# The low-rank gate of GLA moves to the start of the kernel and into four column groups; RWKV matmuls alternate between row groups

## The chip, the cores and the metric

The kernel runs on one core of one Trainium2 chip. The metric is the device time of one execution in microseconds (us). Names of engines in the traces: PE is TensorE (PEld its weight loads), DVE is VectorE, ACT is ScalarE, POOL is GpSimd, SP is the queue that issues the loads and stores.

## The reference

One layer of a hybrid decoder with 1024 tokens and model width 1024, all in fp32. One normalised input is projected once and its columns go to three token mixers, whose outputs (256 + 512 + 256 columns) go into one output projection; a SwiGLU feed-forward part and a last norm follow.

```python
hn = rms_norm(x, norm1_g[l])
p_rw, p_lru, p_gla = _split(hn @ w_in[l], (RW_PROJ, LRU_PROJ, GLA_PROJ))
y_rw = rwkv7_mixer(p_rw, ...)
y_lru = rglru_mixer(p_lru, ...)
y_gla = gla_mixer(p_gla, ...)
x = x + jnp.concatenate([y_rw, y_lru, y_gla], axis=-1) @ w_out[l]
hn = rms_norm(x, norm2_g[l])
x = x + (jax.nn.silu(hn @ ffn_w_gate[l]) * (hn @ ffn_w_up[l])) @ ffn_w_down[l]
```

Two places of the mixers matter here. RWKV takes decay and rate from two low-rank inputs of 64 columns each:

```python
w_raw = w0 + jnp.tanh(w_lo) @ w_up
decay = jnp.exp(-RW_DECAY_SCALE * jax.nn.sigmoid(w_raw.astype(f32)))
a = jax.nn.sigmoid(a0 + a_lo @ a_up)
```

GLA takes its gate from a low-rank input of 16 columns, `gk_lo`, which is one of the slices of the common projection:

```python
q, k, v, gk_lo, g = _split(p, GLA_SIZES)
log_a = jax.nn.log_sigmoid((gk_lo @ gk_up + gk_b).astype(f32)) / GLA_GATE_NORM
```

## The kernel before

Channels lie on the 128 partitions and tokens along the rows. The sequence is taken in two halves of 512 tokens (h = 0, 1). A half is loaded as eight tiles of 128 channels (`ys[h]`), each is multiplied by the norm's weights g1 and split into a high and a low part (xh, xl, in the type fp32r) by `split_x`; 1/rms of each token (`rstd`) is multiplied in only when a result is copied out of PSUM. Weights are split in the same way (wh, wl). A projection of 128 columns is 24 matmuls of 128x512: wh with xh, wh with xl and wl with xh, for eight tiles of channels (`mm3`, line L133). These are most of the kernel's matmuls, and fill TensorE between the mixers' own.

The mixers are functions that issue their instructions step by step in the order of the list `ORDER`. A step is a letter and a number: R is the projection of RWKV, H its output gate's, l and L projection and mixer of the LRU, P and G projection and mixer of GLA, and for the four groups of RWKV (256 tokens each) a is `rw_prep`, b `rw_inner`, c `rw_chain`, p `rw_post`. S splits the second half, O and F are the output projection of half 0 and the LRU's last norm. `AHEAD` gives steps a priority. A scheduler then puts each engine's instructions in a fixed order from dependences, priorities and its own estimate of durations, so that the order of a step's matmuls in the code is not the order in which they stand on TensorE.

What the change touches: `gla_proj` computes the 16 gate columns with 16 matmuls of 128x32 in fp32r (L504 with xh, L505 with xl; the 32 columns hold the high and the low part of the weights, `wgh`), copies them into the first 32 rows of the tile `sc`, and `gla_mix` multiplies by `gku`, which holds gk_up twice (L518). `rw_prep` computes decay from rows 0 to 63 of `ups` and `pw` (L301, two matmuls of 256 columns) and rate from rows 64 to 127 (L309). `rw_inner` computes scores (L368) and transposes B and K by eight matmuls for each half of the rows (L378). Each of these writes into a bank of PSUM named pi, of which there are two; projections mostly use two banks named mm.

Near the mixers' end there are three chains. The LRU's last norm takes a statistic (L174) for each tile and a division and gelu with table loads on ScalarE (L661, L663), then VectorE (L666) and a cast (L104). RWKV's last group ends with the output gate's matmul (L488), VectorE's product (L489), a cast and a subtraction (L104, L105). Then the output projection of half 1 adds x (reloaded from `x1d` at L826), and a statistic (L813) starts the norm ahead of the feed-forward part (first matmul L861).

## Time and profile before

| | |
|---|---|
| median of 3 runs | 1205.6 us (1205.58 to 1206.74) |
| profiled execution, whole time | 1207.51 us |
| its span | 1205.7 us |
| TensorE clock granted, mean | 0.992 |
| TensorE busy | 1159.4 us, 96% |
| weight loads busy | 906.5 us, 75% |
| VectorE busy | 820.5 us, 68% |
| ScalarE busy | 557.5 us, 46% |
| GpSimd busy | 182.6 us, 15% |

The table is of one execution, whose whole time is 1.8 us more than its span. Startup takes the first 42 us or so, the mixers with their projections go on to 486 us, the output projection of half 1 to 534.5 us, and the feed-forward part starts at 538.83 us. In a timeline a matmul's busy time overlaps the next one's, so the distance from start to start is its price. Brackets behind a row tell how long the engine stood idle before it and which instruction ended the wait.

### The profile page before, as it was taken

The page shows a single profiled execution, that of the slowest core. Times are in us where ns is not written, and L with a number is a line of the kernel's source. Part 1 is how long each engine was busy: PE and PEld are TensorE (multiplying, and loading weights), DVE is VectorE, ACT ScalarE, POOL GpSimd, SP SyncE. Part 2 cuts the span into 40 slices and gives each one's busy share as a digit, 9 for nine tenths or more (in the row PEclk, how much of TensorE's full clock was granted, in tenths as well). Part 3 has the DMA queues.
Part 4 walks back from the last instruction along what each step waited for, and adds up shares of the span by engine and source line. Part 5 has one row for each costly group of instructions (what it writes and reads, how often), then busy time and mean ns, then how long its engine had stood idle before and what let it go on. Part 6 is the DMA issues. An engine that isn't in the chain of part 4 may idle for free.

```text
span 1205.7 us, 18433 instructions
## 1 busy us (share of the span) xinstructions
PE 1159.4 (96%) x6550; PEld 906.5 (75%) x6550; DVE 820.5 (68%) x1513; ACT 557.5 (46%) x972; POOL 182.6 (15%) x141
## 2 busy tenths in 40 slices
PE   8899999999999999988899899999999999999996
PEld 4676667677776677766788778888888878888886
DVE  6878797887759676378978664356655475555775
ACT  7445734864541457365433234333333344444542
POOL 0000000000000000000036455454555400000000
PEclk9999999999999999999999999999999999999998
DMA  9865444343333268873699853245454798665422
GB/s 312 291 231 194 141 147 133 90 157 108 130 123 96 87 219 290 273 258 114 190 324 341 283 194 99 96 131 186 146 176 152 268 357 296 196 194 171 128 88 70
DMA packets 125213, 225.52 MB, mean 187 GB/s; under 512 B 13985, under 2 KB 17345, under 8 KB 125121
## 3 DMA queue, kind: packets, MB, share of 16 engines
q1 hardware_dynamic: 124432, 223.78, 55.1%
q8 instruction: 51, 0.84, 0.3%
q10 hardware_dynamic: 688, 0.57, 0.1%
q14 instruction: 42, 0.34, 0.1%
HBM read 149.84 MB, written 74.45 MB: 186 GB/s over the span
## 4 chain that ended last, share of the span: by engine, by line
PE 62%; DVE 15%; ACT 10%; DMA 9%; issue 3%; SPq 1%; POOL 0%; DVEq 0%; ACTq 0%; POOLq 0%
PE mm L861 24%; PE mm L1124 17%; PE mm L133 12%; DVE x L854 2%; DMA x<-w_dn_dram 2%; DMA wd<-x 1%; PE pi L368 1%; DMA wr<-w_in_dram 1%; DMA wr<-w_gu_dram 1%; ACT L663 1%; DVE wl L105 1%; PE pi L408 1%; DVE x L822 1%; DMA parts<-wl 1%; DVE u L651 1%
## 5 line engine op out<-in xcount | busy, mean ns | idle before, releaser
L133 PE MATMUL mm<-xl,wh 128*128 128x512 f32 x420 | 169.6, 404 | 0.0
L133 PE MATMUL mm<-xh,wh 128*128 128x512 f32 x400 | 162.8, 407 | 3.8 <-ACT wh L104 2.9
L133 PE MATMUL mm<-xh,wl 128*128 128x512 f32 x400 | 163.0, 408 | 0.3 <-DVE wl L105 0.3
L104 ACT CAST wh<-wr 128x512 fp32r<-128x512 f32 x133 | 82.0, 619 | 126.5 <-PE mm L861 37.7
L104 ACT CAST vh<-wr 128x512 fp32r<-128x512 f32 x81 | 50.2, 622 | 103.7 <-PE mm L1124 39.1
L133 PEld LDWEIGHTS mm<-xh,wh 128*128 128x128 f32 x400 | 75.4, 188 | 27.1 <-issue 6.1
L133 PEld LDWEIGHTS mm<-xl,wh 128*128 128x128 f32 x420 | 79.0, 188 | 21.9 <-issue 6.4
L105 POOL TENSOR_TENSOR wl<-wr,wh 128x512 fp32r<-128x512 f32 x36 | 53.0, 1472 | 279.9 <-ACT wh L104 265.2
L133 PEld LDWEIGHTS mm<-xh,wl 128*128 128x128 f32 x400 | 75.3, 188 | 22.6 <-issue 5.8
L1124 PE MATMUL mm<-ft,wh 128*128 128x512 f32 x264 | 81.5, 389 | 0.0
L1124 PE MATMUL mm<-ft,vh 128*128 128x512 f32 x264 | 81.3, 389 | 0.0
L854 DVE TENSOR_TENSOR x<-x 128x512 f32<-128x512 f32 x71 | 57.8, 824 | 29.2 <-DMA x<-hd 15.8
L105 DVE TENSOR_TENSOR wl<-wr,wh 128x512 fp32r<-128x512 f32 x97 | 66.3, 685 | 14.2 <-ACT wh L104 13.7
L417 POOL MEMSET ri<- 128x256 f32 x8 | 2.5, 312 | 391.3 <-DVE ri L402 389.3
L1124 PEld LDWEIGHTS mm<-ft,wh 128*128 128x128 f32 x264 | 49.6, 188 | 10.3
L1124 PEld LDWEIGHTS mm<-ft,vh 128*128 128x128 f32 x264 | 49.5, 188 | 10.2
L105 POOL TENSOR_TENSOR vl<-wr,vh 128x512 fp32r<-128x512 f32 x36 | 50.6, 1406 | 37.6 <-ACT vh L104 36.1
L1124 PE MATMUL mm<-ft,wl 128*128 128x512 f32 x132 | 51.3, 389 | 0.0
L1124 PE MATMUL mm<-ft,vl 128*128 128x512 f32 x132 | 51.3, 389 | 0.0
L104 ACT CAST wh<-ws 128x512 fp32r<-128x512 f32 x33 | 20.4, 622 | 50.9 <-PE mm L861 41.0
L105 POOL TENSOR_TENSOR wl<-ws,wh 128x512 fp32r<-128x512 f32 x27 | 38.4, 1424 | 34.6 <-ACT wh L104 26.9
L105 POOL TENSOR_TENSOR vl<-ws,vh 128x512 fp32r<-128x512 f32 x27 | 37.2, 1376 | 35.7 <-ACT vh L104 35.7
(498 smaller groups left out, 2901.0 us busy)
## 6 DMA issues: line engine op xcount, KB each, us to landing
wr<-w_gu_dram SPq DMA_DIRECT2D x108, 256.0 KB, 3.1
parts<-wh SPq DMA_DIRECT2D x60, 256.0 KB, 3.1
parts<-wl SPq DMA_DIRECT2D x60, 256.0 KB, 3.1
wh<-parts SPq DMA_DIRECT2D x57, 256.0 KB, 2.7
wl<-parts SPq DMA_DIRECT2D x57, 256.0 KB, 2.9
wr<-w_in_dram SPq DMA_DIRECT2D x44, 256.0 KB, 3.9
x<-w_dn_dram SPq DMA_DIRECT2D x44, 256.0 KB, 4.5
wd<-x SPq DMA_DIRECT2D x44, 256.0 KB, 3.9
```

The costliest lines, as they stand in the source:

```text
L104: S.copy(out=hi, in_=src)
L105: lo_eng.tensor_tensor(out=lo, in0=src, in1=hi.bitcast(F32), op=ALU.subtract)
L133: PE.matmul(out=ps, lhsT=ww[:, kk], rhs=xx(k), start=first, stop=last)
L368: PE.matmul(out=pgs[hh][:, n * P : n * P + P], lhsT=BKn[hs(hh), nn, 64 * hh : 64 * hh + 128], rhs=ARn[hs(hh), nn], start=True, stop=True)
L408: PE.matmul(out=ps[hs(hh), n * w : n * w + w], lhsT=lhs(hh, n), rhs=rhs(hh, n), start=True, stop=True)
L417: G.memset(hi(Zt), 0.0)
L651: V.tensor_tensor_scan(out=tt[j], data0=out(i), data1=ig[j], initial=lstate[:, i : i + 1], op0=ALU.mult, op1=ALU.add)
L663: S.activation(out=gate, in_=gate, func=AF.Exp, scale=-0.5)
L822: V.scalar_tensor_tensor(out=xk, in0=xk, scalar=vc("g2", k), in1=rs, op0=ALU.mult, op1=ALU.mult)
L854: eng.tensor_tensor(out=out, in0=a, in1=b, op=op)
L861: PE.matmul(out=ps, lhsT=ww[:, kk], rhs=xx, start=first and kk + i == 0, stop=kk == len(xc) - 1 and i == 2, skip_group_check=True)
L1124: PE.matmul(out=out(m), lhsT=ww[:, m], rhs=xx, start=first and open_(m) and k + i == 0, stop=k == KF - 1 and i == 2, skip_group_check=True)
```

## The change

The gate's projection becomes a function of its own, `gk_proj`, with a step "g": g0 stands first in `ORDER`, g1 right behind R1. It takes x itself in fp32, not its split parts, with weights that are multiplied by g1 once (L190). The eight tiles of channels go into four column groups of 32 columns, so two matmuls add up in each group, and the sum over the four groups is left to `gku`, which now holds gk_up four times in 128 rows. `sc` is used in all its rows, so the zeros that it needs in one corner are written after each use, in `gla_mix`. Loads grow from 64 to 128 KB (w_gk) and from 16 to 64 KB (gku). In `rw_prep` and `rw_inner` both banks are taken at once and the matmuls are issued in turn from the two halves of the rows.

```diff
 ORDER = (
-    "R0 H0 a0 l00 b0 k0 l01 a1 L00 c0 l02 X1 P0 b1 p0 "
-    "G0 l03 S1 L01 R1 a2 F0 c1 b2 p1 l10 H1 a3 l11 "
+    "g0 R0 H0 a0 l00 b0 k0 l01 a1 L00 c0 l02 X1 P0 b1 p0 "
+    "G0 l03 S1 L01 R1 g1 a2 F0 c1 b2 p1 l10 H1 a3 l11 "
     "l13 P1 c2 b3 p2 L10 c3 l12 O0 p3 G1 L11 F1"
...
         ups = cp.tile([P, 512], F32, name="ups")
-        gku = cp.tile([32, P], F32, name="gku")
-        wgh = cp.tile([P, 8, 32], F32R, name="wgh")
+        gku = cp.tile([P, P], F32, name="gku")
+        wgk = cp.tile([P, NK, 32], F32, name="wgk")
         cdec = cp.tile([P, 4], F32, name="cdec")
...
             V.tensor_scalar(out=lgh, in0=vt[:, VEC["lg"] : VEC["lg"] + 4], scalar1=0.5, scalar2=None, op0=ALU.mult)
-            gr = rtt((8, 16))
-            nc.sync.dma_start(out=gr, in_=w_gk)
-            split(wgh[:, :, 0:16], wgh[:, :, 16:32], gr, V)
+            nc.sync.dma_start(out=wgk, in_=w_gk)
+            g1 = vt[:, VEC["g1"] : VEC["g1"] + NK].unsqueeze(2)
+            V.tensor_tensor(out=wgk, in0=wgk, in1=g1.to_broadcast([P, NK, 32]), op=ALU.mult)
 
...
             bonus = y[:, 0:2, 3 + o : 259 + o]
-            psw = prep_ps()
+            psw, psa = prep_ps(), prep_ps()
             for hp in range(2):
-                PE.matmul(out=psw[:, hp * 256 : hp * 256 + 256], lhsT=ups[0:64, hp * P : hp * P + P], rhs=pw[0:64, sl], start=True, stop=True)
+                for ps, r in ((psw, slice(0, 64)), (psa, slice(64, P))):
+                    PE.matmul(out=ps[:, hp * 256 : hp * 256 + 256], lhsT=ups[r, hp * P : hp * P + P], rhs=pw[r, sl], start=True, stop=True)
             sig, cs, av = rtt(), rtt(), rtt()
...
                 V.tensor_tensor_scan(out=cs[:, hp], data0=cc("rs64"), data1=sig[:, hp], initial=0.0, op0=ALU.mult, op1=ALU.add)
-            psa = prep_ps()
-            for hp in range(2):
-                PE.matmul(out=psa[:, hp * 256 : hp * 256 + 256], lhsT=ups[64:128, hp * P : hp * P + P], rhs=pw[64:128, sl], start=True, stop=True)
             for hp in range(2):
...
             BKt = rw.tile([P, 2, 8, 64], F32, name="BKt", bufs=2)
+            pbs = [prep_ps(), prep_ps()]
+            for n in range(8):
+                for hh in range(2):
+                    PE.transpose(out=pbs[hh][:, n * 64 : n * 64 + 64], in_=BKn[hs(hh), n, 64 * hh : 64 * hh + 128], identity=ident[hs(hh), hs(hh)])
             for hh in range(2):
-                pb = prep_ps()
-                for n in range(8):
-                    PE.transpose(out=pb[:, n * 64 : n * 64 + 64], in_=BKn[hs(hh), n, 64 * hh : 64 * hh + 128], identity=ident[hs(hh), hs(hh)])
-                S.copy(out=BKt[:, hh], in_=pb.rearrange("p (n i) -> p n i", i=64))
+                S.copy(out=BKt[:, hh], in_=pbs[hh].rearrange("p (n i) -> p n i", i=64))
 
...
 
+        def gk_proj(h, xs):
+
+            ps = pm.tile([P, HT], F32, name="mm")
+            for i in range(2):
+                for j in range(4):
+                    kk = 4 * i + j
+                    PE.matmul(out=ps[32 * j : 32 * j + 32], lhsT=wgk[:, kk], rhs=ys[h][:, kk, 3:], start=i == 0, stop=i == 1, tile_position=(0, 32 * j), skip_group_check=True)
+            V.tensor_tensor(out=sc.rearrange("p a b -> p (a b)"), in0=ps, in1=xs[2], op=ALU.mult)
+
         def gla_proj(xs, y):
...
             qk = unit("qk", (2, HT))
-            q, k, v, g, gk = qk[:, 0], qk[:, 1], [unit("v0"), unit("v1")], [y[:, 6, 3:], y[:, 7, 3:]], sc[0:32].rearrange("p a b -> p (a b)")
-            ps = pm.tile([P, HT], F32, name="mm")
-            for kk in range(NK):
-                PE.matmul(out=ps[0:32], lhsT=wgh[:, kk], rhs=xh[kk], start=kk == 0, stop=False)
-                PE.matmul(out=ps[0:32], lhsT=wgh[:, kk], rhs=xl[kk], start=False, stop=kk == NK - 1)
-            V.tensor_tensor(out=gk, in0=ps[0:32], in1=rstd[0:32], op=ALU.mult)
+            q, k, v, g, gk = qk[:, 0], qk[:, 1], [unit("v0"), unit("v1")], [y[:, 6, 3:], y[:, 7, 3:]], sc.rearrange("p a b -> p (a b)")
             proj(xs, 16, q)
...
             PE.matmul(out=ps, lhsT=gku, rhs=gk, start=True, stop=True)
+            G.memset(sc[64:128, :, 0:64], 0.0)
             z, e = unit(0), unit(1)
...
         sc = gl.tile([P, 4, P], F32, name="sc")
-        G.memset(sc[64:128, :, 0:64], 0.0)
         state = {"rw": rwS, "gl": glS}
...
                 E[f"xs{h}"] = split_x(h)
+            elif k == "g":
+                gk_proj(h, xs)
             elif k == "R":
...
         tiled(cols),
-        np.ascontiguousarray(w_in[:, 2560:2576].reshape(8, P, 16).transpose(1, 0, 2)),
+        np.concatenate([w_in[:, 2560:2576].reshape(8, P, 16).transpose(1, 0, 2), np.zeros((P, 8, 16), np.float32)], 2),
         np.concatenate([np.concatenate([f("rw_w_up"), f("rw_a_up")], 0), f("rw_g_up")], 1),
         lw,
-        np.concatenate([f("gla_gk_up")] * 2, 0),
+        np.concatenate([f("gla_gk_up"), np.zeros((16, P), np.float32)] * 4, 0),
         tiled(np.concatenate([f("w_out")[:768], swap(f("w_out")[768:], 0)], 0))[:, :, KO],
```

How the scheduler's order moves is seen at three places. The first is the start. VectorE takes the first results of RWKV's projection (pw for decay and rate, pk for keys) out of PSUM, mixes each with its shifted copy (rd), and subtracts low parts of weights (wl); before, from the first result on:

```order
L252 TENSOR_TENSOR pw<-pi,rstd 128x512
L275 TENSOR_TENSOR rd<-pw 128x512
L277 SCALAR_TENSOR_TENSOR pw<-rd,vt,pw 128x512
L252 TENSOR_TENSOR pk<-pi,rstd 128x512
L105 TENSOR_TENSOR wl<-wr,wh 128x512
L275 TENSOR_TENSOR rd<-pk 128x512
L105 TENSOR_TENSOR wgh<-rt,wgh 128x8x16
```

VectorE at the same place now:

```order
L252 TENSOR_TENSOR pw<-pi,rstd 128x512
L275 TENSOR_TENSOR rd<-pw 128x512
L252 TENSOR_TENSOR pk<-pi,rstd 128x512
L277 SCALAR_TENSOR_TENSOR pw<-rd,vt,pw 128x512
L190 TENSOR_TENSOR wgk<-wgk,vt 128x256
L105 TENSOR_TENSOR wl<-wr,wh 128x512
L275 TENSOR_TENSOR rd<-pk 128x512
L277 SCALAR_TENSOR_TENSOR pk<-rd,vt,pk 128x512
L504 TENSOR_TENSOR sc<-mm,rstd 128x512
```

The split of the gate's weights (wgh) is gone. Their product with g1 stands behind both first results and the mixing of pw, and the gate's result (sc) is copied out before the decay goes on. TensorE there now, from the last two of the 48 projections that need no gate (pi) on:

```order
L133 MATMUL pi<-xl_172,wh 128x512
L133 MATMUL pi<-xh_171,wl 128x512
L503 MATMUL mm<-y_100,wgk 32x512 x8
L133 MATMUL mm<-xh_143,wh 128x512
...
L133 MATMUL mm<-xh_151,wl 128x512
L302 MATMUL pi<-pw,ups 128x256 x4
L133 MATMUL mm<-xh_155,wh 128x512
```

Before, 12 projections stood between that last pi and L301. Now L503 comes first, nine projections are between it and decay and rate, and fifteen of the same 24 come behind.

The second place is the last pair of LRU tiles, on TensorE. L174 with a tile u is the statistic, `xl_5014` (before) and `xl_4997` (of the change) are low parts of its second tile's result, xh those of the input projections, L450 and L449 are RWKV's last chain. Before:

```order
L133 MATMUL mm<-xh_4282,wh 128x512
L174 MATMUL px<-u_4937,ct 128x512
L133 MATMUL mm<-xl_4283,wh 128x512
...
L133 MATMUL mm<-xh_4258,wh 128x512
L450 MATMUL pc<-R_4151,Tt 64x64 x4
L133 MATMUL mm<-xl_4259,wh 128x512
...
L133 MATMUL mm<-y_5004,wh 128x512
L465 MATMUL pp<-XR_3762,UV_3202 64x64
...
L133 MATMUL mm<-y_5004,wh 128x512
L133 MATMUL mm<-xl_5014,wh 128x512
```

Now:

```order
L133 MATMUL mm<-xl_4988,wh 128x512
L174 MATMUL px<-u_4910,ct 128x512
...
L133 MATMUL mm<-xl_4991,wh 128x512
L174 MATMUL px<-u_4920,ct 128x512
L133 MATMUL mm<-y_4987,wl 128x512
...
L133 MATMUL mm<-y_4987,wh 128x512 x2
...
L133 MATMUL pi<-y_4987,wl 128x512
L449 MATMUL pc<-R_4133,Tt 64x64 x4
L133 MATMUL mm<-y_4987,wh 128x512 x2
...
L133 MATMUL mm<-xl_4997,wh 128x512
```

Before, input projections (xh) stood behind both statistics, and 35 projections lay between the second one and the first instruction that needs its tile (the one ahead of `xl_5014`). Now the input projections are over ahead of the first statistic, and 22 projections, all of the output projection, stand between the second one and the first that needs its tile (the pair behind L449).

The third place is the output gate of RWKV's last group, on TensorE. `xl_5017` (before) and `xl_5000` (of the change) are the first tile that needs its result. Before:

```order
L133 MATMUL px<-y_5004,wh 128x512
L488 MATMUL pp<-pgl,ups 128x256 x2
L133 MATMUL px<-xl_5005,wh 128x512
L133 MATMUL px<-y_5004,wl 128x512
...
L133 MATMUL px<-y_5004,wl 128x512
L133 MATMUL mm<-y_5004,wh 128x512
L133 MATMUL mm<-xl_5017,wh 128x512
```

Now:

```order
L133 MATMUL px<-xl_4997,wh 128x512
L487 MATMUL pp<-pgl,ups 128x256 x2
L133 MATMUL px<-y_4987,wl 128x512
L133 MATMUL mm<-y_4987,wh 128x512 x2
L133 MATMUL pi<-y_4987,wh 128x512
L133 MATMUL mm<-xl_5000,wh 128x512
```

Before, 23 projections (px) stood between the gate and the first use of its result, now one. Behind it, the statistic ahead of the feed-forward part has 58 projections to cover its chain, where it had 60. The order of the feed-forward part is the same but for single rows.

## Rows read from the trace of the kernel before

**Rows 1.** Windows: length, busy (count) of PE, PEld, DVE, ACT, POOL, clock, DMA, GB/s.

```profile
42.00:486.00 444.00, 437.36 (x3320) 319.16 (x3320) 347.37 (x801) 233.07 (x391) 2.50 (x8) 1.00 0.48 159
486.00:540.00 54.00, 47.40 (x191) 35.53 (x192) 28.06 (x47) 24.45 (x39) 0.00 (x0) 0.98 0.79 280
...
32.80:36.00 3.20, 3.18 (x5) 1.68 (x6) 1.68 (x4) 0.90 (x2) 0.00 (x0) 0.50 1.05 392
```

**Rows 2.** Timeline of TensorE, first instruction of the feed-forward part.

```profile
538.83 0.76 PE L861 MATMUL mm<-q_b21h,vh 128*128 128x512 f32 x1 [4.18 <-ACT ft L803]
```

**Rows 3.** Timeline of TensorE near the start.

```profile
22.23 0.39 PE L133 MATMUL pi<-xh,wl 128*128 128x512 f32 x1
...
32.82 0.80 PE L133 MATMUL mm<-xh,wh 128*128 128x512 f32 x1 [2.74 <-ACT wh L104]
...
42.24 0.50 PE L133 MATMUL mm<-xh,wl 128*128 128x512 f32 x1 [0.35 <-DVE wl L105]
```

**Rows 4.** L504's weight loads (its line's view); two dense starts (timeline).

```profile
L504 PEld LDWEIGHTS mm<-xh,wgh x16: 107/108/112, 108.0 to 329.5; 128*32 128x32 f32 x16
...
112.67 0.39 PE L504 MATMUL mm<-xh,wgh 128*32 128x512 f32 x1
112.90 0.40 PE L505 MATMUL mm<-xl,wgh 128*32 128x512 f32 x1
```

**Rows 5.** Timeline of TensorE, decay and rate of group 0.

```profile
26.43 0.48 PE L301 MATMUL pi<-pw,ups 64*128 64x256 f32 x1 [0.77 <-ACT pw L279]
26.44 0.48 PE L309 MATMUL pi<-pw,ups 64*128 64x256 f32 x1
...
27.50 0.50 PE L133 MATMUL mm<-xh,wl 128*128 128x512 f32 x1
```

**Rows 6.** Timeline of TensorE, column groups (L578) and their follower.

```profile
167.40 0.32 PE L578 MATMUL px<-u 128*32 128x64 f32 x8
167.65 0.50 PE L133 MATMUL mm<-xh,wh 128*128 128x512 f32 x1
```

**Rows 7.** Timeline of VectorE, behind the four of pw and pk.

```profile
26.23 0.68 DVE L105 TENSOR_TENSOR wl<-wr,wh 128x512 fp32r<-128x512 f32 x1
```

**Rows 8.** Timeline of TensorE, decay and rate of group 1.

```profile
131.21 1.13 PE L301 MATMUL pi<-pw,ups 64*128 64x256 f32 x4 [1.10 <-DVE Tt L426]
132.27 0.50 PE L133 MATMUL mm<-xh,wl 128*128 128x512 f32 x1
...
133.86 0.70 PE L309 MATMUL pi<-pw,ups 64*128 64x256 f32 x2
...
134.87 0.70 PE L309 MATMUL pi<-pw,ups 64*128 64x256 f32 x2
```

**Rows 9.** Timeline of ScalarE, the copy that frees the second bank.

```profile
132.33 0.57 ACT L428 COPY MV<-pi 128x512 f32<-128x512 f32 x1
```

**Rows 10.** Timeline of TensorE, scores (L368) and transposes (L378).

```profile
72.61 1.71 PE L368 MATMUL pi<-AR,BK 64*128 64x128 f32 x16
...
174.88 0.71 PE L378 MATMUL pi<-ct,BK 64*128 64x64 f32 x8
...
377.29 1.02 PE L378 MATMUL pi<-ct,BK 64*128 64x64 f32 x16
```

**Rows 11.** Timelines of TensorE and ScalarE, the last LRU pair.

```profile
470.49 1.12 PE L174 MATMUL px<-u,ct 128*128 128x512 f32 x2
...
477.26 1.28 ACT L661 ACT_TABLE_LOAD   x1
...
481.95 0.62 ACT L104 CAST y<-y 128x512 fp32r<-128x512 f32 x1 [0.82 <-DVE y L666]
```

**Rows 12.** Timelines of TensorE, VectorE and ScalarE, the last gate.

```profile
495.93 1.03 PE L488 MATMUL pp<-pgl,ups 128*128 128x256 f32 x4
...
497.00 0.69 DVE L489 TENSOR_TENSOR y<-pp,ro 128x512 f32<-128x512 f32 x1 [1.26 <-PE pp L488]
...
497.72 1.14 ACT L104 CAST y<-y 128x512 fp32r<-128x512 f32 x2 [4.21 <-DVE y L489]
```

## The prediction

> **What bounds the kernel now.** I read the table of windows first [rows 1]. Between 42 and 486 us TensorE is busy 437.36 of 444 us, so in the three mixers a TensorE instruction less is time less, as long as something else stands ready to take its place. Between 486 and 540 it is 47.40 of 54 us: here TensorE waits. The longest of these waits, 4.18 us, stands in front of the feed-forward part and is ended by ScalarE [rows 2]; it is the end of the normalisation of out_proj's result, and 60 projections (L133) are all that covers it. The third window, 32.80 to 36.00, was granted a clock of 0.50, the lower of the two levels (1.2 instead of 2.4 GHz), and it follows an idle stretch of 2.74 us [rows 3]. So a wait of some us in this kernel costs twice: the wait and a slow stretch behind it. The prices below are starting distances in the timeline, since its busy times overlap: a dense 128x512 matmul follows the one before after 0.23 us [rows 4].
>
> **The change part by part.**
>
> *The gate projection, what goes.* Each half had 16 matmuls (L504, L505) at 0.23 us, 16 x 0.23 = 3.68 us [rows 4], without a wait.
>
> *What comes.* 8 fp32 matmuls of 512 columns. An fp32 matmul stands in the trace as two records: two matmuls of 256 columns are four records and take 1.07 us [rows 5], so 0.21 us for 256 columns net of entry and 0.43 for 512. One after the other, 16 records are 6.8 us. Four column groups side by side are 4 x 0.43 = 1.7 us and about 0.15 for entry, 1.85. The trace has such a shape: L578, eight records of 64 columns in column groups, is followed by the next L133 after 0.25 us [rows 6], where eight in a row would take 8 x 0.21 / 4 = 0.42 us and two rounds 0.11 and an entry. It is nearest to side by side; I take 1.85 and keep 6.8 as the other bound. A 128x32 weight load takes 108 ns [rows 4]; if all 16 had to wait for the matmul before them, it would be 1.85 + 16 x 0.11 = 3.6 us.
>
> The Trainium skill, "TensorE: Matmul & The Clock Gate", Part 3, "The mechanism", says that a weight load overlaps running matmuls only if its row group differs, and column groups share all their rows. By that rule the 3.6 us would hold, and both halves together would win 3.5 us less than I reckon, for a total of about 1206. The row on L578 does not bear it out: eight exposed loads would not fit into 0.25 us.
>
> *Second half.* 1.85 - 3.68 = **-1.8 us**.
>
> *First half.* Here the step moves from 108 us into the start, right behind the 48 first projections, the last of which begins at 22.23 [rows 3]. It needs the weights times g1 (L190), which stand on VectorE behind pw, rd, pk and pw again. In the trace the operation behind those four starts at 26.23 [rows 7]; L190 has half of its 512 columns, some 0.4 us, so L503 starts at about 26.7. TensorE, which now does 12 projections in this stretch, stands for 4.2 us. The clock then falls as it did after 2.74 us, and 1.85 us of work take about 3.4: 30.1. Nine projections (2.1), L302 (1.07) and fifteen more (3.4) end at 36.7; these are the 24 projections of one column tile, which are through before the wait that ends at 32.82 today. From there today's TensorE does five records in 3.2 us at the low clock [rows 1], dense 1.2 us, so that it stands as if it had started at 34.8, and has one more wait for weights by 42 us, 0.5 with its entry [rows 3], which the later kernel no longer meets. So the start costs 36.7 - 34.8 - 0.5 = 1.4, and 3.7 go at 108 us: **-2.3 us**. Bounds: -3.7 if waits for weights swallow all of it, +1 if the slow stretch is as long as the idle one. The delay of the decay path (L302 at 32.2 instead of 26.43, and VectorE's L504 of 0.7 ahead of its next step) is covered by 132 instead of 118 projections up to the first transposes. On the load queue w_gk moves ahead of two loads of x and has 64 KB more, gku 48 KB: at 392 GB/s [rows 1] 0.3 us for what is queued behind, under the stand of TensorE; without that cover it is 0.3 us once.
>
> *gku with 128 rows, sc in all rows, the memset.* Same columns, so no time on TensorE and VectorE; GpSimd, which is idle but for 2.50 us of this stretch [rows 1], hides the memset. If it did not, it would be one wait of 0.3 us in each of two groups.
>
> *Decay and rate.* Where the two pairs stand next to each other they already run side by side: L309 starts 10 ns after L301, and both pairs are over in 1.07 us [rows 5]. So is group 2. In group 3 the order still has projections between the pairs. Only group 1 wins: today 1.06 for L301 (it overlaps its follower by 0.07), then twice 0.70 - 0.07 = 0.63 for L309 in two pieces, with six projections and the chain's matmuls between [rows 8], later 1.07 in one piece with two changes of shape less at 0.1 each. That is **-1.4 us**. Both banks must now be free at once: the second is freed by ScalarE's copy at 132.33 + 0.57 [rows 9], the first by VectorE, for which L301 waits 1.10 [rows 8]. The copy is later by some 1.5 us, but 18 instead of 12 projections (+1.4 us) stand ahead of L302; I leave the wait at 1.1 (0.5 to 2).
>
> The Trainium skill, same page and part, also says that matmuls start and end strictly in the order of the program. By that, adjacent pairs would run one after the other today, and alternation would win 1.06 us in groups 0 and 2 as well, some 2.1 us more than in my sum. The row of L309 at 26.44 speaks against it: it starts behind the first record of L301, with three of L301 still to come.
>
> *Transposes of B and K, and L366 around them.* 8 of one row group take 0.71 us, 16 in two row groups 1.02; 16 records of L368 in one row group 1.71 [rows 10]. Group 0 has L366 in two alternating pieces and the 16 transposes in one, instead of three and two: about -1.6. Group 1: 16 in one piece, -0.3. Group 3 had them in one piece, which the order now splits: +0.4. Group 2 as it was. **-1.4 us** (0 to -2).
>
> TensorE's own saving: -2.3 - 1.8 - 1.4 - 1.4 = **-6.9 us**. But the mixers end in chains that don't get shorter, and with 6.9 us less work the order runs out of input projections earlier: 23 projections stood between L488 and the first use of its result, now one.
>
> *Last LRU pair.* Its first statistic (L174) starts at 470.49, the second tile's result is cast at 481.95 + 0.62, 12.1 us later [rows 11]; each tile needs two table loads of 1.28 us on ScalarE. After the change 25 projections (5.8), two statistics (0.9) and two pieces of the chain (1.2), about 7.9 us, stand from that statistic to the chain's L449, which sits behind the second tile's last step on VectorE. From its first table load to its cast a tile takes 481.95 + 0.62 - 477.26 = 5.3. With VectorE free at once the chain is 1.3 (statistic and VectorE's step) + 4.0 (first tile, its first load done ahead) + 5.3 - 0.6 (second tile without cast) + 0.3 (VectorE's step for L449) = 10.3; with the delays of today 12.1 - 0.6 + 0.3 = 11.8. So the wait is 2.4 to 3.9, or 1.5 if the first tile starts early. VectorE has less in front now: **+2.4**.
>
> *The last gate.* From L488 to the first cast half: VectorE 497.00 + 0.69, ScalarE from 497.72, two casts in 1.14, so 498.29, that is 2.4 after 495.93 [rows 12]. Under it are now L487 itself and one projection, 1.1: **+1.3** (1.0 to 1.5).
>
> *Cover at the end.* 58 instead of 60 projections lie behind the statistic that starts the last chain, so it starts 2 x 0.23 later: **+0.5**. The reload of x1d is one pair of weights later on the queue; that adds nothing if it still lands ahead of the statistic, up to 2.5 if not; I take 0.1.
>
> Sum: -6.9 + 2.4 + 1.3 + 0.5 + 0.1 = **-2.6 us**. The profiled execution took 1207.51, of which the span is 1205.7; it is 1.9 above the median of the runs. The sum stands against its rows; from the median I get 1205.6 - 2.6 = **1203.0 us**.
>
> **The rivals.**
>
> *All of it arrives* (chance 0.17). The waits at the mixers' end are hidden, because today's wait of 4.18 [rows 2] and others there shift rather than add: 1205.6 - 6.9 = 1198.7. For it: TensorE is all but full over 444 us. Against: the order leaves one projection behind L487.
>
> *The end eats it* (0.25). LRU wait at 3.9, the reload at 2.5, or a slow clock behind one of these waits, as behind the one before 32.82: 1203.0 + 1.5 + 1.0 = 1205.5, between 1204 and 1207.
>
> *The start isn't made good* (slower, 0.12). L503 idles TensorE for 4.2 us and puts decay 5.8 us later. If the chain of group 0 up to the transposes has no slack, those 5.8 us come again as a wait: 1203.0 + 5.8 = 1208.8. It decides once the waits for the first L344 exceed 5 us. For it: nothing else of the chain gets shorter. Against: 14 more projections (3.2 us) stand ahead of it.
>
> *Column groups take turns or their loads are bare* (0.07). +3.5 to +9.9 (two times 6.8 - 1.85), 1206.5 to 1212.9, 1209.7 in the middle. It tips to slower at 2.6 us in a half more.
>
> *Alternation wins where pairs were adjacent* (0.03). -2.1: 1200.9.
>
> **How the numbers follow.** My case has 0.36, with a range of its own from 1201 to 1204.5. Faster by over 0.2% means under 1203.2 (0.2% is about what a measurement of this kernel tells from no change): of my case 0.24 and 0.12 no change, with the 0.17 and the 0.03, and 0.04 of the end that eats, 0.48. No change, to 1208.0: 0.12 + 0.19 of the end + 0.04 of the start + 0.02 = 0.37, and slower 0.15. The range 1198.5 to 1208 leaves out half of the rival of full arrival, most of the two slow ones: 0.2.
>
> **What the profile will show.** L503: eight matmuls at about 26.7 with a low clock, and at about 320 us in some 1.85 us, starts in fours a few ns apart; starts 0.2 us apart or more would prove me wrong. In group 1 L302 takes 1.07 in one piece. At the end: one wait of 2 to 4 us at a chain matmul or cast of the LRU (L449 or L133), one of 1.3 behind L487, and the last one near 4.2 to 4.7. If the LRU wait is missing, the full saving arrives; if one of over 3 us stands between 45 and 75 us, it was the start.

## The result and the profile after

The changed kernel takes 1223.6 us (median of 4 runs, 1220.1 to 1226.5), the one before 1206.2 on the same chip: ratio 1.0135, 95% interval 1.0104 to 1.0165. It is slower by 17.4 us by these medians and by some 16 by the ratio, where 2.6 us less was forecast, and lies far outside the range. The profiled execution took 1224.19 us, its span is 1222.4, and the clock granted over it was 0.982 instead of 0.992.

The first view is the table of windows, since it tells in which stretch time went. After the change (length, then busy time and count of PE, PEld, DVE, ACT and POOL, granted clock, DMA share, GB/s; the last two rows are the output projection of half 1 and the feed-forward part):

```profile
0.00:42.00 42.00, 35.40 (x124) 21.26 (x125) 26.47 (x51) 26.86 (x57) 0.20 (x4) 0.92 0.88 307
42.00:200.00 158.00, 155.84 (x1122) 116.78 (x1120) 138.35 (x343) 83.35 (x153) 1.55 (x5) 1.00 0.60 197
200.00:245.00 45.00, 37.37 (x345) 23.81 (x343) 28.08 (x55) 27.62 (x41) 0.00 (x0) 0.85 0.17 53
245.00:300.00 55.00, 51.17 (x362) 37.16 (x358) 39.56 (x82) 31.30 (x48) 0.00 (x0) 1.00 0.35 106
300.00:470.00 170.00, 167.13 (x1302) 122.19 (x1302) 120.54 (x292) 78.30 (x129) 1.56 (x5) 0.99 0.44 145
470.00:553.10 83.10, 73.33 (x378) 54.88 (x376) 44.44 (x77) 44.90 (x67) 0.00 (x0) 0.96 0.73 249
553.10:1222.40 669.30, 641.76 (x2929) 532.00 (x2928) 418.34 (x617) 272.15 (x485) 176.55 (x128) 0.99 0.57 191
```

The same view of the kernel before, for the stretches that differ most:

```profile
200.00:245.00 45.00, 44.18 (x392) 31.51 (x389) 33.87 (x68) 29.82 (x52) 0.00 (x0) 1.00 0.34 103
245.00:300.00 55.00, 54.83 (x374) 41.63 (x373) 44.73 (x106) 28.08 (x43) 0.00 (x0) 1.00 0.40 126
...
470.00:534.50 64.50, 61.62 (x289) 45.83 (x288) 33.77 (x58) 34.92 (x49) 0.00 (x0) 1.00 0.81 285
534.50:1205.70 671.20, 641.67 (x2929) 532.20 (x2928) 422.91 (x617) 272.05 (x486) 179.62 (x128) 0.99 0.57 191
```

Three things are to be read here. Between 200 and 245 us TensorE was busy 44.18 of 45 us and is now busy 37.37, at a clock of 0.85: this is where half 0 of the mixers hands over to half 1. The end of the mixers, from 470 us to the last matmul of the output projection, is longer and has more idle time in it. The feed-forward part has no share in this loss (it is 1.9 us shorter).

The table below splits the time up to the last matmul of the output projection in the same way: idle is a window's length less TensorE's busy time, low clock is busy time times (1 - granted clock), both added up over windows of 2 us, and work is what remains. Each cell is idle/low clock in us; the experiments' rows are read further down.

| kernel | ends at | 0-42 | 42-200 | 200-245 | 245-470 | 470-end | work |
|---|---|---|---|---|---|---|---|
| before | 534.5 | 7.8/1.4 | 3.2/0 | 0.8/0 | 2.2/0 | 2.9/0 | 516.3 |
| after | 553.1 | 6.6/2.3 | 2.1/0 | 7.6/4.4 | 6.7/1.7 | 9.8/2.9 | 509.0 |
| e1_gate | 558.8 | 8.1/2.9 | 2.1/0 | 7.6/4.4 | 7.4/5.1 | 9.5/1.7 | 509.8 |
| e2_alternation | 548.6 | 6.0/0 | 5.1/4.9 | 8.2/1.7 | 4.8/0 | 3.3/0 | 514.5 |
| e4_stat_bank | 530.1 | 8.0/1.4 | 2.2/0 | 0.0/0 | 1.3/0 | 6.8/3.0 | 507.3 |
| e5_before_bank | 540.4 | 6.9/0 | 3.0/0 | 0.8/0 | 3.2/0 | 6.0/3.3 | 517.2 |
| e6_gate_bank | 531.3 | 8.0/1.6 | 2.1/0 | 0.0/0 | 1.3/0 | 7.8/1.7 | 508.8 |
| e7_alternation_bank | 560.9 | 6.7/1.7 | 5.4/0 | 2.8/0 | 4.4/3.3 | 14.7/5.5 | 516.4 |
| e9_rms_ahead | 542.2 | 8.5/2.9 | 2.2/0 | 6.3/3.6 | 0.0/0 | 9.4/3.2 | 506.2 |

So TensorE's work did fall, by 7.3 us. Idle time and low clock rose by 25.9: 14.8 of that between 200 and 300 us, 9.8 at the end.

**The boundary of the halves.** The projections (L133) alone tell what TensorE lacked. In the windows below the columns are busy (count) of PE and PEld, clock, DMA share and GB/s; first before, then after:

```profile
214.00:225.50 11.50, 5.79 (x19) 3.50 (x19) 1.00 0.19 60
225.50:232.90 7.40, 5.32 (x17) 3.11 (x17) 1.00 0.50 158
```

```profile
214.00:225.50 11.50, 0.08 (x1) 0.00 (x0) 0.85 0.16 47
225.50:232.90 7.40, 0.00 (x0) 0.01 (x1) 0.50 0.08 18
```

Before, 36 projections ran in these 19 us. After, none starts in them (the one counted is the end of the row at 213.68 below). The timeline of TensorE after the change shows what stands there instead (the bracket is the idle time before, and what ended it):

```profile
213.68 0.40 PE L133 MATMUL mm<-xh,wl 128*128 128x512 f32 x1
...
218.09 1.12 PE L174 MATMUL pi<-rt,ct 128*128 128x512 f32 x2 [0.28 <-DVE Tt L425]
220.87 0.45 PE L449 MATMUL pc<-R,Tt 64*64 64x64 f32 x8 [1.66 <-DVE R L446]
226.30 3.75 PE L638 MATMUL px<-u,lw 128*128 128x512 f32 x4 [4.98 <-DVE u L634]
...
231.87 2.08 PE L638 MATMUL px<-u,lw 128*128 128x512 f32 x2 [0.71 <-ACT y L639]
232.96 1.42 PE L133 MATMUL mm<-xh,wh 128*128 128x512 f32 x1
```

The instruction at 218.09 is the statistic from which 1/rms of half 1 is made. It writes into a bank named pi, and VectorE's step that ends its wait (L425) belongs to the inner part of one of RWKV's groups. ScalarE then turns it into 1/rms (L136, L137). After the change, the timelines of ScalarE and VectorE:

```profile
220.63 1.28 ACT L599 ACT_TABLE_LOAD   x1
...
224.43 1.28 ACT L601 ACT_TABLE_LOAD   x1
225.72 1.06 ACT L601 ACTIVATE u_qk<-u_qk 128x1024 f32<-128x1024 f32 x1
226.80 1.28 ACT L136 ACT_TABLE_LOAD   x1
228.09 0.69 ACT L136 ACTIVATE rstd<-pi,vt 128x512 f32<-128x512 f32 x1
...
230.63 0.61 ACT L137 ACTIVATE rstd<-rstd 128x512 f32<-128x512 f32 x1
```

```profile
231.48 0.69 DVE L252 TENSOR_TENSOR pw<-mm,rstd 128x512 f32<-128x512 f32 x1
```

And ScalarE before:

```profile
222.19 0.67 ACT L136 ACTIVATE rstd<-pi,vt 128x512 f32<-128x512 f32 x1
...
224.18 0.63 ACT L137 ACTIVATE rstd<-rstd 128x512 f32<-128x512 f32 x1
```

The statistic itself stood at 218.38 before, so it hardly moved. But ScalarE now first finishes GLA's final norm of half 0 (L599, L601, with a table load each) and makes 1/rms 6.5 us later (230.63 for 224.18). Until then projections of half 1 sit in their banks, because their copy multiplies by `rstd` (the row of VectorE), and new ones have no bank. TensorE has used up the projections that may run before, stands, and is then granted the lower level of the clock, 0.50, in the window from 225.50 to 232.90.

These projections are 576: the 22 column tiles of half 0 and the first two of half 1, 24 matmuls each. The last of them is the row at 213.68 above. Before, it stood 10.7 us later, just behind the start of L137 at 224.18, and the wait behind it was short:

```profile
224.37 0.40 PE L133 MATMUL mm<-xh,wl 128*128 128x512 f32 x1
225.59 0.50 PE L133 MATMUL mm<-xh,wh 128*128 128x512 f32 x1 [0.82 <-DVE pw L252]
```

So the distance from the 576th projection to 1/rms went from nothing to 16.9 us: 10.7 because the order has TensorE through its projections sooner, 6.5 because ScalarE comes to 1/rms later. The mixers' own matmuls fill all but 7.6 us of the stretch. The long wait in the rows, 4.98 us, ends with a step of the LRU (u, L634) and not with 1/rms itself: no projection is left to stand in between.

### The profile page after: what moved, and what is told of

Its sections match the earlier page's. It is cut to its first block, busy times and chain, and to the rows that moved or that the text cites. A ratio compares the mean times of both kernels' runs of the same rounds, so it can differ in the third digit from the quotient of the medians.

```text
span 1222.4 us, 18444 instructions
## 1 busy us (share of the span) xinstructions
PE 1162.0 (95%) x6550; PEld 908.1 (74%) x6550; DVE 815.8 (67%) x1513; ACT 564.5 (46%) x976; POOL 179.9 (15%) x142
## 4 chain that ended last, share of the span: by engine, by line
PE 70%; DVE 12%; DMA 8%; ACT 6%; issue 2%; SPq 1%; DVEq 0%; ACTq 0%
PE mm L866 23%; PE mm L133 18%; PE mm L1129 17%; DMA x<-w_dn_dram 3%; DVE x L859 2%; DMA wr<-w_gu_dram 2%; PE pi L407 1%; PE pi L366 1%; DMA wd<-x 1%; PE px L638 1%; DVE ws L859 1%; PE px L133 1%; PE pi L133 1%; DMA wh<-parts 1%; PE px L574 1%
## 5 line engine op out<-in xcount | busy, mean ns | idle before, releaser
L133 PE MATMUL mm<-xl,wh 128*128 128x512 f32 x420 | 170.1, 405 | 0.0
L133 PE MATMUL mm<-xh,wh 128*128 128x512 f32 x400 | 162.9, 407 | 0.0
L133 PE MATMUL mm<-xh,wl 128*128 128x512 f32 x400 | 161.6, 404 | 0.6 <-DVE wl L105 0.6
L133 PEld LDWEIGHTS mm<-xl,wh 128*128 128x128 f32 x420 | 79.6, 189 | 21.0 <-issue 4.4
L133 PEld LDWEIGHTS mm<-xh,wh 128*128 128x128 f32 x400 | 75.8, 189 | 23.6 <-issue 7.2
L133 PEld LDWEIGHTS mm<-xh,wl 128*128 128x128 f32 x400 | 75.9, 190 | 20.9 <-issue 3.9
```

Of the source, the lines that this page charges most:

```text
L133: PE.matmul(out=ps, lhsT=ww[:, kk], rhs=xx(k), start=first, stop=last)
```

## The experiments

First theory: the saving is spent at the boundary of the halves, since a fixed order of instructions lets TensorE use up its projections before 1/rms of half 1 exists. Rivals: the idle start is carried on through the kernel; the new forms of matmul cost more than reckoned; the loads at the end are what decides.

### The two parts alone

*e1_gate* has the gate's part of the change alone, `rw_prep` and `rw_inner` as before; *e2_alternation* has the alternation alone, with the gate as before.

```diff
 # e1_gate, against the changed kernel
-            psw, psa = prep_ps(), prep_ps()
+            psw = prep_ps()
...
-            pbs = [prep_ps(), prep_ps()]
...
+                pb = prep_ps()
```

```diff
 # e2_alternation, against the kernel before
-            psw = prep_ps()
+            psw, psa = prep_ps(), prep_ps()
...
+            pbs = [prep_ps(), prep_ps()]
...
-                pb = prep_ps()
```

> The changed kernel with its gate projection (columns groups, first step, second step behind R1) but with decay, rate and the transposes of B and K issued as before. Theory 1, the boundary of the halves: TensorE uses up the 48 projections of half 1 that may run before its 1/rms, and ScalarE computes that 1/rms only behind GLA's final norm; the order here has both, so waits of 6 to 8 us stand between 215 and 236 us with a low clock behind, and the time is 1214 to 1222 us. Theory 2, the start: it is the stand of TensorE before the gate at 22 to 26 us that is carried along; also 1214 to 1222 us, but without long waits near 220. Theory 3, taking two banks at once for the alternating matmuls holds the chain up: then this kernel lies near 1203 us.

> The kernel before with decay, rate and the transposes of B and K alternating, and the gate projection as it was (16 matmuls, in its old place). Theory 1 (boundary of the halves): the order has the same place, 1/rms of half 1 behind GLA's final norm with all 48 projections used up, so 6 to 8 us of waits between 215 and 240 us, a low clock behind, and 1212 to 1220 us, although no matmul got dearer and the start is as it was. Theory 2 (the start): no loss, 1203 to 1206 us. Theory 3 (two banks at once): 1212 to 1222 us, but with the time lost at L302 and the transposes.

Measured: 1221.9 us, ratio 1.0133 (1.0069 to 1.0198), and 1217.5 us, 1.0086 (1.0057 to 1.0115). Each part alone makes the kernel slower, and the two losses do not add up to that of the whole. In both, the boundary is the largest new loss (7.6/4.4 and 8.2/1.7 in the table), though other stretches come close to it: from 245 to 470 us e1_gate loses 12.5 us where 2.2 were lost before, and from 42 to 200 us e2_alternation loses 10.0 for 3.2. The waits of TensorE in e2_alternation (total, times, longest) begin with the one of the changed kernel at 226.30 (L633 here is L638 there):

```profile
PE px L633 <- DVE u L629: 5.0, 1, 5.0
```

That kernel has the old start and the old gate. So the idle start is not what is carried on to the boundary, and it takes no L503 to get the wait.

### The gate's steps at their old place

*e3_old_place* keeps the new form of the gate and puts both steps right ahead of GLA's projections.

```diff
-    "g0 R0 H0 a0 l00 b0 k0 l01 a1 L00 c0 l02 X1 P0 b1 p0 "
-    "G0 l03 S1 L01 R1 g1 a2 F0 c1 b2 p1 l10 H1 a3 l11 "
-    "l13 P1 c2 b3 p2 L10 c3 l12 O0 p3 G1 L11 F1"
+    "R0 H0 a0 l00 b0 k0 l01 a1 L00 c0 l02 X1 g0 P0 b1 p0 "
+    "G0 l03 S1 L01 R1 a2 F0 c1 b2 p1 l10 H1 a3 l11 "
+    "l13 g1 P1 c2 b3 p2 L10 c3 l12 O0 p3 G1 L11 F1"
```

> The changed kernel with both gate projections moved back to their old place, right before GLA's projections of each half; column groups, alternation and everything else as changed. Its order has 1/rms of half 1 on ScalarE ahead of GLA's final norm. Theory 1 (boundary of the halves): no wait of over 2 us between 200 and 240 us, and 1200 to 1208 us. Theory 2 (the start): the start is as before, also 1200 to 1206 us. Theory 3 (two banks at once): still 1214 us or more. Theories 1 and 2 are told apart by the second run, not by this one.

Measured: 1254.0 us, 1.038 (1.0338 to 1.0422). At that place the gate reads tiles of x that the LRU's projections have overwritten by then, so it computes another gate and must come behind those projections. It is a miss and answers another question than it was made for. TensorE had no wait at all from 200 to 245 us, but it stood 11.7 us between 42 and 200, with 15.0 us more lost to the clock, 12.7 between 300 and 470 and 19.4 at the end. The time says nothing about the theory, but the boundary does: 1/rms of half 1 was made no earlier than 227.90 (L137), and no wait followed, since TensorE was so late by then that its 576th projection stood at 244.88.

### The statistic in another bank

*e4_stat_bank* is the changed kernel with the statistic of half 1 in a bank that RWKV's groups use for their results (pp), so that it need not wait for pi. *e5_before_bank* is the same edit in the kernel before.

```diff
-                ps = head_sum(acc, ones, prep_ps if h else mix_ps)
+                ps = head_sum(acc, ones, post_ps if h else mix_ps)
```

> The changed kernel with one edit: the statistic of half 1's first norm is summed into the bank pp instead of pi, so that it need not wait for RWKV's inner step to free a pi bank. Its order has 1/rms of half 1 right behind the first group's output gate on ScalarE and ahead of GLA's final norm. Theory 1 (boundary of the halves): the waits of 7.6 us between 218 and 232 us and the low clock behind them go, 10 us less: 1211 to 1215 us, with the waits at the mixers' end (LRU, weights) left. Theory 2 (the start) and theory 3 (two banks at once): as the changed kernel, 1219 to 1226 us.

> The kernel before with the one edit of the bank alone: half 1's first statistic is summed in bank pp instead of pi. Theory 1 (the change lost its time at the boundary of the halves, where 1/rms came too late): before, the wait there was only 0.8 us, so the bank alone gives 0 to 2 us: 1203 to 1206. Rival theory, the bank is a gain of its own that has nothing to do with the change (pi is the crowded bank): 1194 to 1199 us, as with the change.

Measured: e4_stat_bank 1195.4 us, 0.9897 (0.9858 to 0.9936), 28 us less than the changed kernel; e5_before_bank 1211.9, 1.0032 (1.0011 to 1.0053). ScalarE in e4_stat_bank:

```profile
210.22 0.69 ACT L136 ACTIVATE rstd<-pp,vt 128x512 f32<-128x512 f32 x1 [5.98 <-PE pp L174]
...
212.21 0.63 ACT L137 ACTIVATE rstd<-rstd 128x512 f32<-128x512 f32 x1
```

and its projections (windows of L133):

```profile
214.00:225.50 11.50, 6.97 (x29) 5.23 (x29) 1.00 0.30 93
225.50:232.90 7.40, 5.39 (x23) 4.01 (x22) 1.00 0.68 211
```

1/rms is there 18.4 us earlier, 52 projections run where none did, and the loss of 12.0 us between 200 and 245 is gone, although the 576th projection stands at 213.68 as in the changed kernel. That settles the place, and that the late 1/rms is its cause. It doesn't settle the size: the profiled spans differ by 29.7 us, and of those 12.0 are this stretch; 7.1 lie between 245 and 470, 2.9 at the end and 6.7 in the feed-forward part, 1.7 is work, and the first 200 us are 0.6 worse. e5_before_bank says that the bank by itself is no gain: where there is no wait at the boundary, the edit only draws another order, and here a worse one. (e5_before_bank to e8_start_pool ran on another chip than the other experiments; the kernel before took 1206.3 us there and 1206.5 to 1206.8 here.)

Nor is the gain over the kernel before one of the mixers alone. The span of e4_stat_bank is 13.0 us shorter than that kernel's, 4.4 up to the last matmul of the output projection and 8.6 in the feed-forward part, which none of the edits touches. There TensorE stood 21.8 us instead of 29.5 (to be read against the row from 534.50 above):

```profile
530.10:1192.70 662.60, 640.84 (x2929) 530.97 (x2928) 418.63 (x609) 270.73 (x483) 178.66 (x128) 0.99 0.58 193
```

No run tells why. In the kernels of the table this part takes between 661.5 (e6_gate_bank) and 671.2 us (before), and it is as short in e1_gate, which is slow in all (661.9).

### The parts alone, with the bank

*e6_gate_bank* is e1_gate and *e7_alternation_bank* e2_alternation, both with this edit:

```diff
-                ps = head_sum(acc, ones, prep_ps if h else mix_ps)
+                ps = head_sum(acc, ones, post_ps if h else mix_ps)
```

> Gate projection changed, bank pp for half 1's statistic, no alternation. By my terms the gate is worth 4.1 us and the alternation 2.8, both on TensorE inside the mixers: theory 1 expects 2 to 4 us more than the run with everything and the bank (1195.4), so 1197 to 1200. Rival theory (the bank is the gain): as the kernel before with the bank, within 1 us.

> Alternation changed, bank pp for half 1's statistic, gate projection as before. Theory 1: 3 to 5 us more than with everything and the bank: 1198 to 1201 us. Rival theory (the bank is the gain): as the kernel before with the bank, within 1 us.

Measured: e6_gate_bank 1195.6 us, 0.9898 (0.9873 to 0.9923), and e7_alternation_bank 1225.8, 1.0156 (1.0128 to 1.0184), a clear miss. With the bank, the gate's part alone reaches the whole gain, and the alternation adds nothing to it (0.2 us, within the spread of the runs). Of the 12.9 us by which the span of e6_gate_bank is shorter than before, 9.7 lie in the feed-forward part, so the gain is not shown to be the gate's own saving. In e7_alternation_bank the boundary lost only 2.8 us, but the end lost 20.2 and the stretch before it 7.7; its longest wait is for a cast that the output projection reads:

```profile
PE mm L133 <- ACT y L104: 7.2, 1, 7.2
```

So the first theory holds for the boundary, and only there. What the order does at the end of the mixers is a matter of its own.

### The weights' product on GpSimd

*e8_start_pool* is e4_stat_bank with the product of the gate's weights and g1 on GpSimd.

```diff
-            V.tensor_tensor(out=wgk, in0=wgk, in1=g1.to_broadcast([P, NK, 32]), op=ALU.mult)
+            G.tensor_tensor(out=wgk, in0=wgk, in1=g1.to_broadcast([P, NK, 32]), op=ALU.mult)
```

> Everything changed, bank pp for half 1's statistic, and the product of the gate's weights with g1 on GpSimd instead of VectorE, so that it waits for its load alone and not behind four operations on VectorE. My step on the start says that TensorE's stand of 4.2 us and the low clock behind it cost 1.4 us net: expected 1 to 3 us less than with VectorE (1195.4), so 1192 to 1195, with the gate's matmuls at about 23 us and no clock of 0.50 behind them. Rival: the start is covered by waits for weights anyway, so within 0.5 us of 1195.4.

Measured: 1194.0 us, 0.9901 (0.9872 to 0.9929). L503 of half 0 starts at 24.09 after 1.42 us idle, and takes 1.92 us, where e4_stat_bank had 26.12, 4.18 and 3.33, the last at the lower clock. The start lost 6.1/0 instead of 8.0/1.4, that is 3.3 us less, and the whole kernel 1.4 us by the medians, with runs that overlap: 1.7 us are lost again between 245 and 470 and 1.4 at the end of the mixers. With e6_gate_bank, these two are the fastest versions of this study.

### The 1/rms ahead of GLA's norm, in the old bank

*e9_rms_ahead* is the changed kernel with GLA's final norm of half 0 made to depend on 1/rms of half 1, so that ScalarE must do that first; for this, step G0 moves behind S1. The constant that it adds (a zero times `rstd`, plus the same epsilon) leaves the values as they are.

```diff
-    "G0 l03 S1 L01 R1 g1 a2 F0 c1 b2 p1 l10 H1 a3 l11 "
+    "l03 S1 G0 L01 R1 g1 a2 F0 c1 b2 p1 l10 H1 a3 l11 "
...
-                S.activation(out=r[:, i], in_=ps, func=AF.Ln, bias=vc("eps6"), scale=1.0 / 64)
+                if y is ys[0]:
+                    ee = gl.tile([P, 1], F32, name=f"ee{i}")
+                    V.scalar_tensor_tensor(out=ee, in0=E["xs1"][2][:, 0:1], scalar=0.0, in1=vc("eps6"), op0=ALU.mult, op1=ALU.add)
+                S.activation(out=r[:, i], in_=ps, func=AF.Ln, bias=ee if y is ys[0] else vc("eps6"), scale=1.0 / 64)
```

> The changed kernel, half 1's statistic still in bank pi, but GLA's final norm of half 0 is made to depend on half 1's 1/rms (the norm's small constant is passed through one element of it, times zero, plus the constant), so that ScalarE must compute 1/rms first. TensorE's order is that of the changed kernel up to the 576th projection. Theory 1 (boundary of the halves: 1/rms comes 6.6 us late because ScalarE does GLA's norm with two table loads first): 1/rms is ready at about 226 instead of 231 us, the projections go on at about 227 instead of 233, and 5 us or more are won: 1214 to 1219 us. Rival (the place on ScalarE does not matter, it is the statistic's bank or the number of projections left): 1/rms is earlier, but the time stays at 1221 to 1226.

Measured: 1208.6 us, 1.0009 (0.9989 to 1.003), 15 us less than the changed kernel and more than expected. 1/rms comes 4.1 us earlier than there, and the first projection behind it 4.3. Its timelines of ScalarE and TensorE:

```profile
226.53 0.61 ACT L137 ACTIVATE rstd<-rstd 128x512 f32<-128x512 f32 x1
```

```profile
228.63 0.80 PE L133 MATMUL mm<-xh,wh 128*128 128x512 f32 x1
```

But the stretch from 200 to 245 still loses 6.3/3.6, only 2.1 us less. The statistic is where it was (218.92), and ScalarE takes it 5.1 us later (L136 at 223.99). The bank and ScalarE's order can't be weighed against each other by this run, since 4.1 us earlier is not enough. In e4_stat_bank both come together: of its 18.4 us, 9.0 are the statistic (209.05 for 218.09), and the rest is ScalarE, which takes it after 1.2 us instead of 10.0. Most of the 15 us came later, between 245 and 470, where this order has no idle time at all (8.4 us less).

The two starts that decide at the boundary, side by side for all kernels, with the loss from the table (idle and low clock together; e3_old_place as read above):

| kernel | 576th projection | 1/rms of half 1 (L137) | lost from 200 to 245 us |
|---|---|---|---|
| before | 224.37 | 224.18 | 0.8 |
| after | 213.68 | 230.63 | 12.0 |
| e1_gate | 214.66 | 231.61 | 12.0 |
| e2_alternation | 220.14 | 239.96 | 9.9 |
| e3_old_place | 244.88 | 227.90 | 0 |
| e4_stat_bank | 213.68 | 212.21 | 0 |
| e5_before_bank | 225.88 | 213.53 | 0.8 |
| e6_gate_bank | 214.91 | 213.45 | 0 |
| e7_alternation_bank | 220.54 | 219.88 | 2.8 |
| e9_rms_ahead | 214.52 | 226.53 | 9.9 |

Where 1/rms starts ahead of the 576th projection, at most 2.8 us are lost; where it starts 12 to 20 us behind it, 9.9 to 12.0.

### The loads at the end

The end after the change, in TensorE's timeline:

```profile
499.88 0.45 PE L449 MATMUL pc<-R,Tt 64*64 64x64 f32 x8 [2.49 <-DVE R L446]
...
506.74 0.50 PE L133 MATMUL pi<-y,wh 128*128 128x512 f32 x1 [2.67 <-DMA wh<-parts]
518.37 0.73 PE L133 MATMUL mm<-y,wh 128*128 128x512 f32 x2 [1.21 <-ACT y L104]
530.26 0.79 PE L133 MATMUL pi<-y,wh 128*128 128x512 f32 x1 [3.39 <-DMA wh<-parts]
557.10 0.77 PE L866 MATMUL mm<-q_b21h,vh 128*128 128x512 f32 x1 [3.87 <-ACT ft L808]
```

Two waits of 2.67 and 3.39 us for weights of the output projection had not been forecast, and the second is followed by a stretch at the lower clock. The windows of the changed kernel show why loads are late:

```profile
490.00:500.00 10.00, 7.50 (x42) 5.09 (x40) 4.58 (x10) 7.68 (x10) 0.00 (x0) 1.00 0.10 37
...
505.00:510.00 5.00, 3.26 (x13) 2.48 (x14) 0.00 (x0) 1.65 (x2) 0.00 (x0) 1.00 0.81 277
...
525.00:530.00 5.00, 1.87 (x9) 1.21 (x7) 2.45 (x4) 3.09 (x5) 0.00 (x0) 0.93 1.05 394
530.00:535.00 5.00, 4.74 (x11) 3.73 (x12) 2.34 (x4) 1.94 (x4) 0.00 (x0) 0.50 1.06 388
```

From 490 to 500 us the DMA engines moved 37 GB/s (213 before, in the same window), and 30 us later they are full. The load queue stood in between, with a load of raw feed-forward weights (L848) at its head. *e10_load_queue* puts the first eight of those loads on GpSimd's queue.

```diff
-            nc.sync.dma_start(out=raw, in_=src)
+            (nc.gpsimd if turn["r"] <= 8 else nc.sync).dma_start(out=raw, in_=src)
```

> The changed kernel with the first eight loads of raw feed-forward gate weights issued by GpSimd instead of the sync queue, so that out_proj's weights don't stand behind a load that waits for a buffer. Orders on TensorE are the same up to the mixers' end. Theory: the two waits for weights at 506.7 (2.67) and 530.3 us (3.39, with 2.5 us at the low clock behind it) come from the 10.9 us that the sync queue stands for a buffer at 490 to 501 us; without them 5 to 8 us less: 1215 to 1219 us. Rival: the loads are bound by the DMA engines there, so at most 1 us less.

Measured: 1221.8 us, 1.0119 (1.0087 to 1.0151); 1.8 us less than the changed kernel, inside the spread of its runs. What SP's queue waited for between 484 and 525 us (total, times, longest), after the change and then in e10_load_queue:

```profile
SPq L848 <- DVE vl L105: 10.9, 1, 10.9
```

```profile
SPq L115 <- PE mm L133: 11.7, 2, 11.1
```

With the load of raw weights out of the way, the next one, a load of weights for the output projection (L115), stands for just as long: its buffer is still held for a projection on TensorE. The first wait for weights is down to 0.49 us in this run (at 505.15), but the second is up to 5.52 (at 530.73), so nothing is won. The load at the head of the queue was not the cause: the queue waits for TensorE, which waits for the last groups of the mixers.

*e11_best_start_queue* and *e12_bank_queue* put the same edit on e8_start_pool and e4_stat_bank:

```diff
-            nc.sync.dma_start(out=raw, in_=src)
+            (nc.gpsimd if turn["r"] <= 8 else nc.sync).dma_start(out=raw, in_=src)
```

> Everything changed, statistic in bank pp, product of the gate's weights on GpSimd, and the first eight feed-forward loads issued by GpSimd. If the three edits add up (10 us from the boundary, 1 to 3 from the start, some of the waits at the mixers' end): 1189 to 1194 us. If the end is bound by the chains there and not by loads: 1193 to 1196.

> Everything changed, statistic in bank pp, first eight feed-forward loads issued by GpSimd, product of the gate's weights on VectorE as changed. In the run with the bank alone only 0.9 us are waited for weights at the mixers' end, so the queue should bring 0 to 2 us: 1193 to 1196 us.

Measured: 1198.6 us, 0.9928 (0.9903 to 0.9954), and 1199.0, 0.993 (0.9903 to 0.9957): 4.6 and 3.5 us worse than without it by the medians (runs of e8_start_pool and e11_best_start_queue overlap). The other queue is no gain anywhere.

## Why the prediction was wrong

**What was right.** The form of the gate: the start, half 1 and group 1 of RWKV in TensorE's timeline.

```profile
26.25 3.64 PE L503 MATMUL mm<-y,wgk 128*32 128x512 f32 x16 [4.32 <-DVE wgk L190]
...
32.58 1.14 PE L302 MATMUL pi<-pw,ups 64*128 64x256 f32 x8
...
133.97 1.14 PE L302 MATMUL pi<-pw,ups 64*128 64x256 f32 x8 [0.40 <-DVE Tt L425]
...
275.04 1.92 PE L503 MATMUL mm<-y,wgk 128*32 128x512 f32 x16
277.10 0.45 PE L344 MATMUL pi<-ct,pv 64*64 64x64 f32 x8
```

- *Second half of the gate*, forecast 1.85 us: 16 records in 1.92, 2.06 to the next start. The first four start within 20 ns (275.044 to 275.064): four column groups run side by side. The rule of the Trainium skill, "TensorE: Matmul & The Clock Gate", Part 3, "The mechanism", that a weight load overlaps matmuls only if its row group differs, would have given 3.6: the trace does not agree here. The gate came at 275, not at the 320 of the forecast.
- *Start*, forecast L503 at 26.7 after 4.2 us idle and at a low clock: 26.25, 4.32, and 3.64 us of busy time for what takes 1.92 later. The price was 1.4; by the table the start loses 0.3 us less than before [rows 3]. The rival "The start isn't made good" did not happen: the stretch from 42 to 200 us is 1.1 us better.
- *Group 1 of decay and rate*: one piece, 1.14 [rows 8], and a wait of 0.40 instead of 1.1. In group 0 it is 1.14 as well, and the next matmul follows at 33.65, after 1.07, as before [rows 5]: where the pairs were adjacent, alternation wins nothing.
- *TensorE's saving.* The terms without the start's cost make 3.7 + 1.8 + 1.4 + 1.4 = 8.3; the table has 7.3.
- *Last LRU pair*, +2.4: a wait of 2.49 at L449. *Last gate*, +1.3: 1.21 behind L487. *The feed-forward part's wait*, 4.2 to 4.7: 3.87 [rows 2].

**The step that failed** is the first paragraph's: that in the mixers "a TensorE instruction less is time less, as long as something else stands ready to take its place". That condition is the part that was wrong. It was taken as met from 42 to 486 us because TensorE was busy 437 of 444 us there [rows 1], and was looked into only at the start and at the end. But that view tells of the order before, not of the one after. The boundary of the halves is a second end: what may run ahead of 1/rms of half 1 is limited to 576 projections, like what is left at the mixers' end. There the order after the change is as different as at the three places that were shown, and neither a term nor a rival had it: the 576th projection stands 10.7 us earlier, 1/rms 6.5 us later. Against the sum: TensorE's work -7.3, start -0.3, 42 to 200 us -1.1, 200 to 300 us **+14.8**, 300 to 470 us +2.6, the end **+9.8**, which is +18.5; the feed-forward part gave 1.9 back, and the span is 16.7 longer.

**The second one** is at the end. Its two waits were forecast in place and size (3.7 of the 9.8 us), but transfers were priced at 0.1 as a reload "one pair of weights later". They cost 2.67 and 3.39 us and the slow stretch of 2.9 behind. With the two waits that were forecast that makes 12.7, and 2.9 is what the same stretch lost before. As the rows of the end read, a wait of TensorE holds weight buffers as well, so the loads behind it come late and then all at once (no run freed those buffers, so this link is read and not tested); a term for a wait near the end of a loop has to have its transfers too. "The end eats it" was the nearest rival, and with 2.5 us on top of the sum too small by far.

**What stays open.** Each edit draws a new order of all engines, so no experiment holds the rest of the kernel still. Why the change of a bank is worth 28 us and not the 12 that it frees at its place; why the same edit costs 5.6 us in the kernel before (1211.9 for 1206.3) and 8.4 in e2_alternation; why the feed-forward part is shorter by up to 9.7 us in kernels that leave it as it is. The stretches in which these differ are known, and that each has another order. Which decision of the scheduler leads to which wait was not tried.

## What to carry to other kernels

Where a program fixes each engine's order ahead of time, a saving on the engine that bounds it arrives only up to the next point at which its filler work is limited by a result that did not get earlier. Look for all such points, the boundaries between halves as well as the end, and compare the new order at each: how much filler stands there, and when the result that releases more of it comes. If it comes late, bring that result forward (here a small statistic in another bank: 12 us at the boundary, 28 in all) before saving more work. With it the changed kernel was 1% faster than the one before, without it 1% slower; but two thirds of that 1% came in a part that nobody had changed, so a gain has to be looked up stage by stage as well as a loss.

## What the runs showed of the hardware

The granted clock after an idle stretch was not the same for like lengths. After 2.67 us of waiting at 506.74 it stayed at 1.00 (window 505 to 510), where the kernel before had 0.50 after 2.74 us at 32.82 [rows 3], and after 3.39 us at 530.26 it was 0.50 again. So a wait's second price, the slow stretch, can't be read from the length of the wait alone: the prediction charged it at the start, where it came, and its sum had no term for it at the boundary of the halves and at the end, where it cost 4.4 and 2.9 us; only the rival "The end eats it" named it.
